# Weights rounded on ScalarE and their rest taken on VectorE, with a list scheduler that treats the path of VectorE and GpSimd as exclusive

## The chip, the cores and the metric

One NeuronCore of a Trainium2 chip runs the whole program in one launch. The metric is the device time in microseconds of that core, the median of several executions. TensorE is PE in the profile, VectorE DVE, ScalarE ACT, GpSimd POOL, and SyncE, which issues the DMAs, SP.

## What is computed

Two blocks of two layers each work on 512 tokens of 1024 features; the second has a context of 256 tokens beside them. In outline, from the reference:

```python
for l in range(2):                          # first block
    u = rms_norm(h, attn_norm[l])
    (dq, dk, dv, rq, rk, rv, rg, gq, gk, gv, gate_logits) = split(u @ w_in[l])
    a, r, c = differential_attention, bidirectional_retention, grouped_query_attention
    h = h + sum(sigmoid(gates) * projected(a, r, c)) @ w_out[l]
    h = h + square(relu(rms_norm(h, mlp_norm[l]) @ w_mlp_in[l])) @ w_mlp_out[l]
for l in range(2):                          # second block
    mx = split(silu(c) @ w_mod[l] + b_mod[l])          # the modulation, also for the context
    z = modulate(rms_norm(x, norm1_g[l]), mx[0], mx[1]) @ w_in_2[l]
    y = concat(fourier_mix, latent_attention, conformer_conv)   # of parts of z; 31 taps in the convolution
    x = x + mx[2] * (y @ w_o[l])
    x = x + mx[5] * mlp(modulate(rms_norm(x, norm2_g[l]), mx[3], mx[4]))
return rms_norm(x, final_norm_g)
```

## The kernel before

Features lie on the partitions and tokens in the columns. Every product is made of fp32r parts: an operand is split into a rounded part (hi) and the rest (lo), and three matmuls, hi by hi, hi by lo and lo by hi, are summed in PSUM. A weight comes as a chunk of 128 x 1024 fp32 (512 KB) into one of three `raw` tiles, is rounded into one `w` tile, and its rest goes into another (six `w` tiles, so three weights at a time). `wload` (L589) does that. For each weight in turn it takes the next letter of HI and of LO (L57, L58): by these, every second weight is rounded on ScalarE with its rest taken on VectorE, and the others are rounded and reduced on GpSimd:

```python
if HI[turn[0] % len(HI)] == "P":
    G.tensor_scalar(out=wh, in0=raw, scalar1=1.0, scalar2=0.0, op0=ALU.mult, op1=ALU.add)
else:
    S.activation(wh, raw, AF.Copy)
lo(wl, raw, wh, G if LO[turn[0] % len(LO)] == "P" else V)
```

A full weight serves 24 matmuls of 512 columns for the 512 tokens.

The program has eight phases (`phase`, L1670): for each layer of the first block a mixer (three kinds of attention, `mixer1`) and an output projection with the MLP (`mlp`, L808), then the same for the second block (`mixer2`). Beside the MLPs of the first block, VectorE makes the modulation of the second (`modulation`, L1224): for 48 chunks of the modulation's weights, one product with a row sum for each of one or two vectors (tiles `mraw` and `junk`). In the second block's mixers VectorE makes the convolution's taps (`taps`, L1299; tiles `cu` to `h`): 25 of the 31 for each of two feature blocks, the others being shared by ScalarE and GpSimd. In the attention (`attend`, L1455) VectorE takes the score's minimum (`s<-sc`) and the rests of the split weights (`r<-mm,r`), ScalarE the exponential and GpSimd the division. The rests of squares for the norms (`squares`, L651; tile `x`) lie mostly on GpSimd, and so do the squares of the MLP's hidden layer.

Nobody writes the order down by hand. The code records its steps, and at the end of a phase `Sched.run` (L270) orders them by a list scheduler: it simulates the five engines with a duration for each step (`_cost`, L484), gives each free engine its ready step of the lowest priority number, the number following the recorded order, and lets `hold` (L360) keep an engine free for a more urgent step that is about to come. Each engine's steps go on its queue in that order, and each waits for its inputs in the queue. In the model of before, VectorE and GpSimd do not hinder each other.

Of the kernel before, what the change touches and what calls it, by code (L numbers as in the profile page):

```python
# [56 lines left out]
HI = "AP"  # L57
LO = "VP"  # L58
# [26 lines left out]
class Buf:  # L85
    """A tile to be placed in one of its tag's slots."""
# [8 lines left out]
class View:  # L95
    """An access pattern on a Buf: the steps from the slot's tile, and what they give on the first slot."""
# [22 lines left out]
    def region(self):  # L119
        """bounds of the partitions and columns"""  # L120
        (pitch, n), *free = self.proto.ap
        p, c = divmod(self.proto.offset, pitch)
        return p, p + n, c, c + 1 + sum(abs(s) * (k - 1) for s, k in free)
# [8 lines left out]
class Op:  # L132
    __slots__ = ("eng", "calls", "cost", "prio", "idx", "bufs", "deps", "nexts", "ready", "unstarted", "soon", "allocs", "frees", "done", "line", "t0", "tr", "why", "rel", "slots", "outs")


class Tag:
# [4 lines left out]
    def take(self, pinned):  # L141
        """a free slot; what is kept beyond the phase goes into none of the phase's own"""
        for s in self.free:
            if (s in self.extra) != pinned:
                self.free.remove(s)
                return s
        return None if pinned else self.free.pop(0)


class Sched:  # L150
    """Records instructions on the engines, orders them by a model of the engines' time, issues them in that order."""

    def __init__(self, tc):
        self.tc, self.nc = tc, tc.nc
        self.tags, self.ops, self.bufs, self.bias, self.macro = {}, [], [], 0.0, None
        self.behind, self.dma = {}, 0.0
# [50 lines left out]
    def group(self):  # L207
        """the calls inside are one step of one engine"""
# [10 lines left out]
    def ahead(self, n):  # L219
        """the steps inside come before those recorded up to n steps earlier"""  # L220
# [11 lines left out]
    def _add(self, calls):  # L232
        op = Op()
        op.eng, op.calls, op.cost, op.idx = calls[0][0], calls, 0.0, len(self.ops)
        writes, reads, deps = [], [], {}
        for eng, name, a, k in calls:
# [7 lines left out]
            op.cost += _cost(eng, name, out, ins, k)  # L244
        for b, r in reads:
            deps.update((o.idx, o) for o, q in b.written if _meet(q, r))
        starts = any(k.get("start") for _, _, _, k in calls)
        for b, r in writes:
            # sums in one bank of PSUM come one after the other
# [20 lines left out]
    def run(self):  # L270
        """order and issue what has been recorded"""
        ops = self.ops
        total = len(ops)
        # how many slots of a tag are taken at each step of the recorded order
# [12 lines left out]
        if LS:  # L287
            # the latest start at which the tensor engine would not wait, were it to go in the recorded order
# [25 lines left out]
        ready = {e: [] for e in self.engines}  # L314
        events, order, now, dma = [(t, 0, 0) for t in sorted({0.0, *free_at.values()})], [], 0.0, self.dma
# [7 lines left out]
        def fits(b):  # L323
            """a slot is free, and taking it leaves enough for the steps before"""
# [35 lines left out]
        def hold(op):  # L360
            """when to look again, if a step that matters more comes before this one would be through"""
# [10 lines left out]
        while left:  # L372
            for e in self.engines:
                if free_at[e] > now:
                    continue
                while ready[e]:
# [6 lines left out]
                    if place(op):  # L383
# [4 lines left out]
                        else:  # L388
                            end = free_at[e] = now + op.cost
# [54 lines left out]
        # what is still under way when the tensor engine is through  # L444
        base = free_at["PE"]
        self.behind, self.dma = {e: max(0.0, t - base) for e, t in free_at.items()}, max(0.0, dma - base)
        for b in {id(b): b for b in self.bufs}.values():
            b.at = max(0.0, b.at - base)
# [34 lines left out]

def _cost(eng, name, out, ins, k):  # L484
    """an instruction's time in us, about"""
    n = max([_free_size(out)] + [_free_size(x) for x in ins if name in ("reduce_max", "tensor_reduce")])
    ps = any(_in_psum(x) for x in ins)
    if eng == "PE":
        if name == "transpose":
            return 0.115  # L490
        return n / 2400 + 0.0025 if n >= 256 else 0.22
# [16 lines left out]
def kernel(  # L508
# [80 lines left out]
    def wload(src, n=1024):  # L589
        """hi and lo of weights"""  # L590
# [17 lines left out]
    def prefetch(srcs):  # L608
        """weights for the next phase"""
# [6 lines left out]
    def gemm(w, off, nk, streams):  # L616
        """streams: (psum, hi blocks, lo blocks); w: hi and lo with block k at column off + k * 128."""
# [10 lines left out]
    def rstd(ms, eps, n=T):  # L628
        """-16/3 / sqrt(ms + eps) for rows that are alike: a guess from the bits, a step of third and one of second order on one copy"""
# [16 lines left out]
    def colsum(ps, m, x, start=True, stop=True):  # L646
        """the product of the symmetric constant m with x, given as its parts"""
# [39 lines left out]
    def qcol(p, name, n, scale):  # L687
        """gains of queries whose products are the negated scores"""
# [4 lines left out]
    def softmax(ps, e):  # L693
        """of the negated scores; less than normalized by the returned factor"""
# [10 lines left out]
    def sumsq(src, n):  # L705
        """the squares of all blocks but the last, summed"""
# [8 lines left out]
    def factor(most, last, n):  # L715
        """of the norm, from the squares' sum and the last block"""
# [5 lines left out]
    def operand(n):  # L722
        """hi and lo tiles of a block, kept until they are unpinned"""
# [5 lines left out]
    def cut(n):  # L729
        """the columns in halves, as far as they are more than 256"""  # L730
        return [slice(c, c + TC) for c in range(0, n, TC)]

    def scaled(y, x, gain, R, b):
        """x times its norm's factor; some of the blocks on another engine"""
# [7 lines left out]
    def norm_split(src, gains, n, shifts=None, over=False, later=None):  # L742
        """over: src is not needed any more; later: what is left to do for the last columns is put here"""
# [36 lines left out]
    def sweep(ws, streams, done, first=0, last=0):  # L780
        """products of each of the weights with the streams (hi blocks, lo blocks, n); done(unit, stream, columns, psum).
        The first units take the columns in halves as they come; the last ones finish one half before the other."""
# [953 lines left out]
    src = xT  # L1736
# [214 lines left out]
```

## Time and profile before

| | |
|---|---|
| runs shown | 3695.89, 3703.10, 3703.23 us; median 3703.1 |
| span of the profiled execution | 3698.5 us, 46918 instructions; the profile gives no other time of its own for it, and the three runs lie on both sides |
| mean granted clock of TensorE | 0.965 |
| PE | 3398.3 us busy (92%) |
| DVE | 2291.2 us (62%) |
| ACT | 1205.4 us (33%) |
| POOL | 1883.2 us (51%) |
| DMA | 324.48 MB, mean 88 GB/s |

Busy times are sums over the whole span, and the stages differ: an engine with a mean of 62% can be full in one of them. The first block's mixers run to about 620 and 1655 us, their MLPs to about 1060 and 2090; the second block's mixers, the third and the fourth, run to about 2400 and 3270, their MLPs to about 3030 and the end. All work is issued from one helper, so every row carries line L443; the rows are told apart by their tiles, with buffer numbers left out.

### The profile page before, as it was taken

The page shows a single profiled execution, that of the slowest core. Times are in us where ns is not written, and L with a number is a line of the kernel's source. Part 1 is how long each engine was busy: PE and PEld are TensorE (multiplying, and loading weights), DVE is VectorE, ACT ScalarE, POOL GpSimd, SP SyncE. Part 2 cuts the span into 40 slices and gives each one's busy share as a digit, 9 for nine tenths or more (in the row PEclk, how much of TensorE's full clock was granted, in tenths as well). Part 3 has the DMA queues.
Part 4 walks back from the last instruction along what each step waited for, and adds up shares of the span by engine and source line. Part 5 has one row for each costly group of instructions (what it writes and reads, how often), then busy time and mean ns, then how long its engine had stood idle before and what let it go on. Part 6 is the DMA issues. An engine that isn't in the chain of part 4 may idle for free. (4 is left out here: it accounts for less than half of the span.)

```text
span 3698.5 us, 46918 instructions
## 1 busy us (share of the span) xinstructions
PE 3398.3 (92%) x17724; PEld 2852.2 (77%) x17724; DVE 2291.2 (62%) x3816; ACT 1205.4 (33%) x2467; POOL 1883.2 (51%) x1350
## 2 busy tenths in 40 slices
PE   6999899899989998998999978899999987889998
PEld 5777677777877776777778867788888886878887
DVE  7777774998267778748842599852222259953223
ACT  3444332211234443333112326832111222742122
POOL 5544556554454445556544566643333346754445
PEclk9999999999989999999999989999999998999999
DMA  3221124454331211234743201121121221022332
GB/s 108 69 65 53 57 69 143 152 193 161 103 107 58 67 57 58 69 106 146 247 140 102 99 30 36 45 64 63 59 68 58 68 71 61 24 69 91 97 97 80
DMA packets 100308, 324.48 MB, mean 88 GB/s; under 512 B 11120, under 2 KB 18288, under 8 KB 100080
## 3 DMA queue, kind: packets, MB, share of 16 engines
q1 hardware_dynamic: 100080, 321.48, 26.2%
q8 instruction: 139, 2.28, 0.3%
q14 instruction: 89, 0.73, 0.1%
HBM read 312.00 MB, written 9.44 MB: 87 GB/s over the span
## 5 line engine op out<-in xcount | busy, mean ns | idle before, releaser
L443 PE MATMUL mm<-r,w 128*128 128x512 f32 (+2 forms) x12095 | 2604.5, 366 | 115.3 <-DVE r L443 50.2
L443 PEld LDWEIGHTS mm<-r,w 128*128 128x128 f32 (+1 forms) x12095 | 2060.2, 193 | 473.2 <-DVE r L443 60.3
L443 POOL TENSOR_TENSOR w<-raw,w 128x1024 fp32r<-128x1024 f32 (+1 forms) x232 | 676.4, 2915 | 725.7 <-PE mm L443 720.4
L443 DVE TENSOR_TENSOR w<-raw,w 128x1024 fp32r<-128x1024 f32 (+1 forms) x234 | 362.8, 1551 | 456.7 <-PE mm L443 406.1
L443 POOL TENSOR_SCALAR w<-raw 128x1024 fp32r<-128x1024 f32 (+1 forms) x232 | 268.0, 1155 | 534.0 <-PE mm L443 492.3
L443 ACT ACTIVATE w<-raw 128x1024 fp32r<-128x1024 f32 (+1 forms) x234 | 244.7, 1046 | 903.3 <-PE mm L443 662.8
L443 POOL TENSOR_SCALAR e<-e,s 128x512 f32<-128x512 f32 (+1 forms) x176 | 155.0, 885 | 176.6 <-DVE s L443 166.4
L443 ACT ACTIVATE e<-sc,s 128x512 f32<-128x512 f32 (+2 forms) x208 | 153.8, 741 | 144.2 <-DVE s L443 142.9
L443 DVE TENSOR_REDUCE s<-sc 128x1 f32<-128x512 f32 (+2 forms) x208 | 152.9, 741 | 36.8 <-PE sc L443 35.4
L443 PE MATMUL mm<-rc,w 128*128 128x256 f32 x768 | 166.1, 280 | 0.0
L443 PEld LDWEIGHTS mm<-rc,w 128*128 128x128 f32 x768 | 139.7, 188 | 20.5 <-POOL w L443 0.2
L443 DVE SCALAR_TENSOR_TENSOR mraw<-mraw,mrow 128x1024 f32<-128x1024 f32 x96 | 146.8, 1538 | 11.1 <-DMA mraw<-in_wmod_dram 7.8
L443 DVE SCALAR_TENSOR_TENSOR h<-cu,half,h 128x512 f32<-128x512 f32 (+1 forms) x144 | 151.7, 1083 | 1.5
L443 ACT ACTIVATE r<-t 128x512 fp32r<-128x512 f32 (+2 forms) x143 | 83.9, 592 | 141.5 <-DVE t L443 124.9
L443 PE MATMUL mm<-r,r 128*128 128x256 f32 (+1 forms) x592 | 115.5, 327 | 11.2 <-DVE r L443 8.1
L443 POOL TENSOR_TENSOR t<-t,t 128x512 f32<-128x512 f32 (+2 forms) x70 | 90.5, 1297 | 68.3 <-DVE t L443 44.7
L443 PE MATMUL mm<-x,sums 128*128 128x512 f32 (+1 forms) x152 | 62.9, 434 | 65.6 <-DVE sums L443 16.8
L443 ACT ACTIVATE r<-mm 128x256 fp32r<-128x256 f32 (+1 forms) x276 | 94.4, 404 | 72.9 <-PE mm L443 67.2
L443 PE MATMUL mm<-w,r 128*128 128x256 f32 x720 | 110.1, 298 | 8.2 <-DVE r L443 4.9
L443 ACT ACTIVATE t<-mm 128x512 f32<-128x512 f32 (+4 forms) x126 | 67.6, 538 | 150.3 <-PE mm L443 138.1
L443 DVE SCALAR_TENSOR_TENSOR junk<-mraw,mrow 128x1024 f32<-128x1024 f32 x64 | 116.1, 1815 | 0.6 <-DMA mraw<-in_wmod_dram 0.6
L443 DVE TENSOR_TENSOR r<-mm,r 128x256 fp32r<-128x256 f32 (+1 forms) x270 | 105.6, 432 | 10.9 <-ACT r L443 10.0
(586 smaller groups left out, 4511.7 us busy)
## 6 DMA issues: line engine op xcount, KB each, us to landing
raw<-in_wm_dram SPq DMA_DIRECT2D x256, 512.0 KB, 3.6
raw<-in_win_dram SPq DMA_DIRECT2D x134, 512.0 KB, 3.6
mraw<-in_wmod_dram SPq DMA_DIRECT2D x96, 512.0 KB, 4.1
raw<-in_wbr_dram SPq DMA_DIRECT2D x24, 512.0 KB, 3.5
raw<-in_wout_dram SPq DMA_DIRECT2D x16, 512.0 KB, 3.7
raw<-in_wo_dram SPq DMA_DIRECT2D x16, 512.0 KB, 3.4
kept<-h SPq DMA_DIRECT2D x24, 256.0 KB, 2.1
h<-kept SPq DMA_DIRECT2D x24, 256.0 KB, 4.6
```

The source lines that it names most:

```text
L443: getattr(self.engines[eng], name)(*[_real(x) for x in a], **{n: _real(x) for n, x in k.items()})
```

## The change

It has two parts. HI and LO lose their letter P: no weight is rounded or reduced on GpSimd any more; all are rounded on ScalarE, and all rests are taken on VectorE. And the scheduler keeps a time at which the common path of VectorE and GpSimd is free: a step that uses it starts in the model no earlier than that, and holds it to its end. By the new `_port`, every GpSimd step but a memset uses it, and on VectorE a step with two wide inputs in SBUF, or one of a few kinds with all inputs and the output in SBUF. TensorE's durations in the model change slightly too. The rest of the diff takes out comments and unused slots.

```diff
-HI = "AP"
-LO = "VP"
+HI = "A"
+LO = "V"
...
-        self.behind, self.dma = {}, 0.0
+        self.behind, self.dma, self.port = {}, 0.0, 0.0
...
+            op.port = op.port or _port(eng, name, out, ins)
...
+        port = self.port
...
-                            end = free_at[e] = now + op.cost
+                            end = free_at[e] = (max(now, port) if op.port else now) + op.cost
+                            if op.port:
+                                port = end
...
+        self.port = max(0.0, port - base)
...
+def _port(eng, name, out, ins):
+    if eng == "POOL":
+        return name != "memset"
+    if eng != "DVE" or name in ("memset", "reciprocal", "transpose", "stream_shuffle", "tensor_reduce", "reduce_max"):
+        return False
+    wide = [x for x in ins if not _in_psum(x) and _free_size(x) > 1]
+    return len(wide) > 1 or (len(wide) == len(ins) and not _in_psum(out) and name in ("tensor_scalar", "tensor_copy", "scalar_tensor_tensor"))
...
         if name == "transpose":
-            return 0.115
-        return n / 2400 + 0.0025 if n >= 256 else 0.22
+            return 0.11
+        return 0.009 + n * 0.000426 if n >= 256 else 0.22
```

The order on the engines, counted over the whole program: steps that write a weight's tile go from 234 to 466 on ScalarE, from 234 to 466 on VectorE and from 464 to none on GpSimd. No other kind of step is added or taken away on any engine; the matmuls are the same 17726 rows.

**VectorE beside the first MLP's second half of units** (`w<-raw,w` is a weight's rest, `mraw` and `junk` the modulation's products, `h<-h,mm` the residual's sum). Before:

```order
L443 TENSOR_TENSOR w_102<-raw_108,w_103 128x1024
L443 SCALAR_TENSOR_TENSOR mraw_4419,mod0c<-mraw_4419,mrow_4423 128x1024
L443 SCALAR_TENSOR_TENSOR junk_4424,mod0x<-mraw_4420,mrow_4422 128x1024
L443 TENSOR_TENSOR r_70<-t2x,r_71 128x512
L443 SCALAR_TENSOR_TENSOR mraw_4420,mod0c<-mraw_4420,mrow_4423 128x1024
L443 TENSOR_TENSOR h_139<-h_139,mm_4415 128x512
L443 SCALAR_TENSOR_TENSOR junk_4424,mod0x<-mraw_4421,mrow_4422 128x1024
L443 SCALAR_TENSOR_TENSOR mraw_4421,mod0c<-mraw_4421,mrow_4423 128x1024
L443 TENSOR_TENSOR w_106<-raw_108,w_107 128x1024
```

With the change:

```order
L447 TENSOR_TENSOR w_107<-raw_109,w_102 128x1024
L447 TENSOR_TENSOR h_142<-h_142,mm_4416 128x512
L447 SCALAR_TENSOR_TENSOR mraw_4420,mod0c<-mraw_4420,mrow_4423 128x1024
L447 SCALAR_TENSOR_TENSOR junk_4424,mod0x<-mraw_4421,mrow_4422 128x1024
L447 SCALAR_TENSOR_TENSOR mraw_4421,mod0c<-mraw_4421,mrow_4423 128x1024
L447 TENSOR_TENSOR w_103<-raw_110,w_106 128x1024
L447 TENSOR_TENSOR h_140<-h_140,mm_4417 128x512
L447 SCALAR_TENSOR_TENSOR junk_4424,mod0x<-mraw_4419,mrow_4422 128x1024
L447 SCALAR_TENSOR_TENSOR mraw_4419,mod0c<-mraw_4419,mrow_4423 128x1024
L447 SCALAR_TENSOR_TENSOR junk_4424,mod0x<-mraw_4420,mrow_4422 128x1024
L447 TENSOR_TENSOR w_107<-raw_108,w_105 128x1024
```

Before, a rest stood after every five products or so; now one stands after every two or three, and each residual's sum has one beside it. From the first product of this phase to its last stood 19 rests before and 46 now, so the 96 products are spread over more weights. In the second such phase (64 products) it is 15 and 33.

On GpSimd, where a rounding and a rest of a weight stood between the squares of the hidden layer, only the squares are left.

**VectorE in the third mixer, where the first score comes** (`h<-cu,half,h` a tap, `s<-sc` a score's reduction, `s<-s` a reciprocal, `q0l`, `q1l` and `r<-mm,r` parts of queries and of transposed scores). Before:

```order
L443 SCALAR_TENSOR_TENSOR h_145<-cu_14085,half,h_145 128x256
L443 SCALAR_TENSOR_TENSOR h_142<-cu_14084,half,h_142 128x256
L443 TENSOR_TENSOR r_100<-mm_14074,r_100 128x256
L443 SCALAR_TENSOR_TENSOR h_145<-cu_14085,half,h_145 128x256
L443 SCALAR_TENSOR_TENSOR h_142<-cu_14084,half,h_142 128x256
L443 SCALAR_TENSOR_TENSOR h_145<-cu_14085,half,h_145 128x256
L443 TENSOR_REDUCE s_133<-sc_14072 128x1
L443 TENSOR_REDUCE s_131<-sc_14073 128x1
L443 RECIPROCAL s_127<-s_134 128x1
```

With the change:

```order
L447 TENSOR_REDUCE s_127<-sc_14072 128x1
L447 TENSOR_TENSOR w_102<-raw_109,w_107 128x1024
L447 RECIPROCAL s_131<-s_129 128x1
L447 TENSOR_REDUCE s_123<-sc_14073 128x1
L447 TENSOR_REDUCE s_136<-sc_14072 128x1
L447 SCALAR_TENSOR_TENSOR h_140<-cu_14082,half,h_140 128x512
L447 RECIPROCAL s_135<-s_133 128x1
L447 SCALAR_TENSOR_TENSOR h_141<-cu_14083,half,h_141 128x512
L447 RECIPROCAL s_137<-s_125 128x1
L447 TENSOR_REDUCE s_128<-sc_14073 128x1
L447 TENSOR_TENSOR r_83<-mm_14077,r_72 128x2x128
```

Before, 80 of this mixer's 96 two-input taps stood ahead of the first score's reduction; now it is 37, and the other 59 stand among the 48 reductions, the last of them behind 38. In the fourth mixer, with 48 taps and 32 reductions, 41 stood ahead, and now 32 do.

## Rows read from the trace of the kernel before

**Rows 1.** The page, busy time by engine: us, share of the span, instructions.
```profile
PE 3398.3 (92%) x17724; PEld 2852.2 (77%) x17724; DVE 2291.2 (62%) x3816; ACT 1205.4 (33%) x2467; POOL 1883.2 (51%) x1350
```

**Rows 2.** Busy time by stretch: stretch and its us, engines, clock, DMA share, GB/s.
```profile
92.00:555.00 463.00, 435.35 (x2057) 339.39 (x2056) 350.41 (x653) 185.45 (x387) 233.04 (x159) 0.98 0.19 63
692.00:842.00 150.00, 132.51 (x569) 107.88 (x569) 147.64 (x166) 28.63 (x40) 73.95 (x38) 0.95 0.58 199
1760.00:1900.00 140.00, 122.88 (x506) 98.29 (x506) 109.71 (x132) 22.39 (x30) 65.70 (x32) 0.93 0.66 225
2117.00:2400.00 283.00, 229.74 (x1475) 200.84 (x1474) 266.02 (x508) 158.49 (x392) 187.68 (x176) 0.93 0.12 37
3055.00:3268.00 213.00, 176.72 (x1095) 155.16 (x1093) 196.50 (x338) 116.55 (x274) 147.86 (x120) 0.91 0.14 45
3346.00:3677.00 331.00, 331.00 (x1522) 276.72 (x1523) 83.66 (x95) 74.80 (x111) 169.91 (x103) 1.00 0.30 94
```

**Rows 3.** Weights: groups by shape (all), then durations in ns, 3345 to 3676.
```profile
L443 DVE TENSOR_TENSOR w<-raw,w 128x1024 fp32r<-128x1024 f32 x228 | 357.8, 1570 | 456.7 <-PE mm L443 406.1 <-issue 40.3 <-ACT w L443 10.1
L443 ACT ACTIVATE w<-raw 128x1024 fp32r<-128x1024 f32 x228 | 241.7, 1060 | 903.3 <-PE mm L443 662.8 <-DMA raw<-in_wm_dram 192.8 <-DMA raw<-in_win_dram 12.7
...
L443 DVE TENSOR_TENSOR w<-raw,w x31: 1224/1226/2811, 3344.6 to 3661.7; 128x1024 fp32r<-128x1024 f32 x31
...
L443 POOL TENSOR_TENSOR w<-raw,w x31: 2412/3146/3317, 3344.8 to 3668.2; 128x1024 fp32r<-128x1024 f32 x31
L443 POOL TENSOR_SCALAR w<-raw x30: 1055/1057/1378, 3351.7 to 3667.0; 128x1024 fp32r<-128x1024 f32 x30
```

**Rows 4.** Timeline: one collision of VectorE and GpSimd (start us, us, engine).
```profile
807.34 2.05 DVE L443 TENSOR_TENSOR w<-raw,w 128x1024 fp32r<-128x1024 f32 x1
808.28 3.37 POOL L443 TENSOR_TENSOR w<-raw,w 128x1024 fp32r<-128x1024 f32 x1
809.32 3.40 DVE L443 SCALAR_TENSOR_TENSOR mraw<-mraw,mrow 128x1024 f32<-128x1024 f32 x1
...
812.65 1.21 DVE L443 SCALAR_TENSOR_TENSOR junk<-mraw,mrow 128x1024 f32<-128x1024 f32 x1
...
813.80 0.68 DVE L443 TENSOR_TENSOR r<-t2x,r 128x512 fp32r<-128x512 f32 x1
```

**Rows 5.** Groups by shape, 690 to 850: VectorE, then GpSimd.
```profile
L443 DVE SCALAR_TENSOR_TENSOR junk<-mraw,mrow 128x1024 f32<-128x1024 f32 x34 | 61.8, 1817 | 0.0
L443 DVE SCALAR_TENSOR_TENSOR mraw<-mraw,mrow 128x1024 f32<-128x1024 f32 x34 | 50.7, 1491 | 0.5
L443 DVE TENSOR_TENSOR w<-raw,w 128x1024 fp32r<-128x1024 f32 x13 | 24.3, 1872 | 3.9 <-issue 3.9
...
L443 POOL TENSOR_TENSOR w<-raw,w 128x1024 fp32r<-128x1024 f32 x12 | 35.8, 2985 | 31.6 <-PE mm L443 31.6
```

**Rows 6.** TensorE's waits: 692 to 842; 1760 to 1900; 1665 to 1760; all.
```profile
PE mm L443 <- DVE r L443: 11.0, 3, 4.7
PE mm L443 <- DVE w L443: 6.5, 2, 4.9
...
PE mm L443 <- DVE r L443: 14.8, 6, 5.1
...
PE mm L443 <- POOL w L443: 5.6, 2, 2.8
...
PE mm L443 <- POOL x L443: 14.8, 15, 3.0
```

**Rows 7.** Taps: 2117 to 2400, 3055 to 3268; then score reductions, 2200 to 2420.
```profile
L443 DVE SCALAR_TENSOR_TENSOR h<-cu,half,h 128x512 f32<-128x512 f32 x48 | 51.6, 1100 | 0.8
L443 DVE SCALAR_TENSOR_TENSOR h<-cu,half,h 128x256 f32<-128x256 f32 x48 | 38.0, 823 | 0.4
...
L443 DVE SCALAR_TENSOR_TENSOR h<-cu,half,h 128x512 f32<-128x512 f32 x48 | 62.2, 1325 | 0.3
...
L443 DVE TENSOR_REDUCE s<-sc x48: 385/939/958, 2257.8 to 2391.8; 128x1 f32<-128x768 f32 x32, 128x1 f32<-128x256 f32 x16
```

More of the change, by code (lines that the diff above doesn't have):

```diff
@@ L132 @@
 class Op:
-    __slots__ = ("eng", "calls", "cost", "prio", "idx", "bufs", "deps", "nexts", "ready", "unstarted", "soon", "allocs", "frees", "done", "line", "t0", "tr", "why", "rel", "slots", "outs")
+    __slots__ = ("eng", "calls", "cost", "prio", "idx", "bufs", "deps", "nexts", "ready", "unstarted", "soon", "allocs", "frees", "done", "rel", "outs", "port")
 class Tag:
@@ L233, in _add @@
         op = Op()
-        op.eng, op.calls, op.cost, op.idx = calls[0][0], calls, 0.0, len(self.ops)
+        op.eng, op.calls, op.cost, op.idx, op.port = calls[0][0], calls, 0.0, len(self.ops), False
         writes, reads, deps = [], [], {}
```

## The prediction

> **What bounds the kernel now.** I began with busy time by engine: TensorE is busy 3398.3 of 3698.5 us, 92% [rows 1]. So nothing outside TensorE can give back more than the 300 us in which it stands, and the question is where these lie and who owes them. The next view was busy time by stretch. In the last MLP, 3346 to 3677, TensorE is busy all 331 us at a granted clock of 1.00, and VectorE 83.66 [rows 2]: half of its weights go through GpSimd there, and none is late. Nothing done to the weights can help such a stretch. In the first attention stage, 92 to 555, TensorE is busy 435.35 of 463 us. The idle time is thick in four other stretches of the same group: 692 to 842 and 1760 to 1900, the MLPs of the first block beside which VectorE computes the modulation, and 2117 to 2400 and 3055 to 3268, the second block's attention with the convolution's taps on VectorE. There VectorE is busy 147.64 of 150, 109.71 of 140, 266.02 of 283 and 196.50 of 213 us. In all four it is the engine to watch, and each names a wait on it below.
>
> **Why VectorE is so full there.** The same instruction has two very different times. The rest of a 1024-column weight on VectorE takes 1570 ns in the mean of 228, while in the last MLP its median is 1226 and its longest 2811; GpSimd's version of it runs from 2412 to 3317 there [rows 3]. The timeline of one collision shows why [rows 4]. VectorE's rest, noted at 807.34, ends at 809.39 although it needs 1.23; GpSimd's rest, noted at 808.28, ends at 811.65, which is some 2.3 after VectorE's end; VectorE's product noted at 809.32 takes 3.40 and ends at 812.72, one 1.2 after GpSimd's end; the next one, with nobody against it, takes 1.21. The two take turns, whole instruction by whole instruction. So in these stretches the thing that fills is their common path, and VectorE's busy time holds its waiting.
>
> **Part 1: 232 weights leave GpSimd.** Each took there a rounding of 1.06 us and a rest of 2.41 at best [rows 3], both through the common path: 3.47 us. Now it takes a rounding of 1.06 on ScalarE, which is busy 28.63 of 150 us in the fullest MLP stretch [rows 2], and a rest of 1.23 on VectorE. ScalarE's share I cost at nothing: its cover is the idle time of an engine that has over 110 us of 150 free, and in the attention of 2117 to 2400, where it is busy 158.49 of 283, nine more roundings are under 10 us. On VectorE the sum is 232 x 1.23 = 285 us of new work, against 3.47 - 1.23 = 2.2 us less on the common path for each weight.
>
> *The two modulation stretches.* From 690 to 850 VectorE's rows are 34 products of 1817 ns, 34 of 1491 and 13 rests of 1872, together 136.8 us, and GpSimd makes 12 rests in 35.8 [rows 5]. Without collisions the 68 products are 68 x 1.21 = 82.3 and the 13 rests 16.0 [rows 4, 3]; with GpSimd's 12 weights at 3.47, 41.6, the common path carries 140 of 160 us before any of the hidden layer's squares and rests. After the change it carries 82.3 + 25 x 1.23 = 113. VectorE itself goes from 136.8 to 113 in these rows though it does 12 rests more, because the long GpSimd instructions that it waited out are gone. The order shows moreover fewer products to a weight. TensorE waits 11.0 + 6.5 us for VectorE in the first of the stretches and 14.8 in the second [rows 6], 32.3 in all. I take three quarters, **-24 us**; the bounds are 0 (products ahead of a rest still hold it up) and -32. Along with it goes a slower clock: the granted clock is 0.95 and 0.93 of full in the two stretches, against 1.00 in the last MLP, where TensorE does not stop [rows 2]. That is at most 0.05 x 150 + 0.07 x 140 = 17 us, much of it in idle time; **-6**, bounds 0 and -17.
>
> *The start of the second such phase.* TensorE waits 5.6 us for two weights that GpSimd makes [rows 6]. Rounded and reduced in 1.06 + 1.23 rather than 1.06 + 2.41, they come earlier; late next are the residual's norm and VectorE's rests. **-4**, bounds 0 and -5.6.
>
> *GpSimd's other work.* In the attention stages it makes the rests of squares, and a weight's 3.47 us stands ahead of them in its queue. TensorE waits 14.8 us for these, 15 times [rows 6]. **-6**, bounds +10 (the 1.23 us rests now stand ahead of VectorE's score work instead) and -14.8.
>
> *The two convolution stretches.* Nine weights leave GpSimd between 2117 and 2400 and eight between 3055 and 3268, by a count of its rests there, three and two of them short: some 9 us of rests more on VectorE in each. The long taps take 1100 and 1325 ns in the mean [rows 7], where a 512-column step with nobody against it takes 0.68 [rows 4]: collisions cost them 48 x 0.42 = 20 us and 48 x 0.65 = 31. GpSimd's weights are about 30 of its 187.68 and 147.86 us [rows 2], a sixth to a fifth, so they caused some 4 and 6 us of that, and about 3 of the short taps'. Part 1 alone costs VectorE about +3 us in each stretch.
>
> **Part 2: the scheduler's model.** With the common path exclusive in its model, the order changes most at the taps. Before, 80 of the 96 taps of the third attention stand on VectorE ahead of its first score reduction, and the clock agrees: the reductions run from 2257.8 to 2391.8 [rows 7], 140 us after the stretch began. Now 37 do, and the other 59 lie between the steps of the attention. 43 taps at about 0.96 us, the mean of 1100 and 823, are 41 us of VectorE that come later. That is no gain by itself, since VectorE bounds both halves; what it can win is VectorE's idle time, 283 - 266.02 = 17 us, and 213 - 196.50 = 16.5 in the fourth attention, where the taps ahead of the first score go from 41 to 32 of 48. I take half, 17, less the 6 of part 1: **-11 us**. Bounds: +26 (the taps hold the scores up) and -40 (half of all the taps' collision time goes too, because the order sends the two engines apart). The longer TensorE step in the model, 0.227 for 0.216 us, moves fill work a little and has no row; nothing, inside these bounds.
>
> **Sum.** -24 - 6 - 4 - 6 - 11 = -51 us on the profiled span of 3698.5: 3647.5. The median of the runs shown, 3703.1, lies 4.6 above that span; the forecast for a median is 3652.
>
> A rule of the Trainium skill speaks against the change. Perfetto Trace Analysis, Optimizing Scalar/DVE Operations, advises, where VectorE is saturated, to take work away to ScalarE or even GpSimd, though it adds that the two share a port so that moving between them might not help. By its first half, bringing rests to a VectorE that is busy nine tenths would cost their whole time, which is the rival S below, +44 us where the sum says -51. The collision of rows 4 speaks for its second half, and I go by the sum.
>
> **The rivals.**
> S, slower: VectorE becomes the bound. It decides if a weight's share of VectorE in the modulation stretches exceeds the 5.3 us in which TensorE uses up a weight (331 us for the 62 whose rests start in the last MLP [rows 2, 3]). With three products, a rest and a 0.68 step it is 3 x 1.21 + 1.23 + 0.68 = 5.5, with two 4.3. The order holds both; over eight weights there are 20 products, 4.9 on average, so the margin is thin, and collisions with GpSimd's remaining squares could eat it. Then the new rests of the two stretches, 12 as GpSimd makes them in the first [rows 5] and as many assumed in the second, cost 1.23 each, 30 us, those of the convolution 18, and only the -4 is kept: +44, **3747**. Against it: the common path gets 27 us of 160 free. 10%.
> N, no change: the waits come from the products' places ahead in VectorE's queue, whoever shares its path. Then the products still hold up rests, the waits of 32.3 us stay, and so does the clock. -4 and -6 are left, and the taps win nothing: **3693**, or 3699 with part 1's 3 us in each of their stretches. For it: VectorE idles under 3 of 150 us. 12%.
> B, a larger gain: the model's order keeps the engines apart everywhere. -32 - 14 - 5.6 - 14.8 - 40 = -106: **3597**. For it: collisions touch nearly every two-input row of VectorE. Against: the order is set from modelled times, and the chip's drift from them. 18%.
>
> **How the numbers follow.** The forecast has 60%. Its bounds do not all fall together; -90 to -10 holds most of it. The range 3600 to 3697 leaves out S and about half of B's cases and a little of N. A measurement of this kernel can tell about 0.2%, 7.4 us, from no change. Faster by more: the forecast, B and nearly half of N, 0.83. Within: half of N and the edge of S, 0.07. Slower: 0.10, from S.
>
> **What would show it.** Right: rests on VectorE near 1.25 us in the mean of 466 and none of a weight on GpSimd; modulation products near 1.25 instead of 1.5 to 1.8; TensorE's waits for VectorE in the first modulation stretch down from 17.5 to under 6, and its clock there near 1; the first score reduction of the third attention some 30 us sooner after the first tap, the last one at most 10 sooner. Wrong: products that stay above 1.5 us, a TensorE that waits for a rest more often than now, or an attention that grows by as much as the taps ahead of it shrink.

## The result, and the profile after

The changed kernel takes 3542.7 us in the median (3539.3 to 3545.9) against 3699.5 (3694.3 to 3703.2) for the kernel before beside it: a ratio of 0.9579, 95% interval [0.9565, 0.9592]. That is 157 us less. The forecast was 51, and the time lies 57 us below the range's lower end.

The page of the changed kernel, busy time by engine (us, share of the span, instructions), beside [rows 1]:

```profile
PE 3348.9 (95%) x17724; PEld 2823.5 (80%) x17724; DVE 2285.2 (65%) x4048; ACT 1437.3 (41%) x2699; POOL 948.2 (27%) x886
```

The profiled span went from 3698.5 to 3537.5, by 161. TensorE's idle time went from 300.2 to 188.6 us, by 111.6, and its busy time, for the same matmuls, by 49.4. The second number is nearly all clock: its mean over the span rose from 0.965 to 0.977, and busy time times clock is 3279 before and 3272 after. VectorE took on 232 more instructions and is busy 6 us less.

Groups by shape of the kernel before, whole span (count, then busy us and mean ns), beside [rows 3] for the weights:

```profile
L443 DVE SCALAR_TENSOR_TENSOR mraw<-mraw,mrow 128x1024 f32<-128x1024 f32 x96 | 146.8, 1538 | 11.1 <-DMA mraw<-in_wmod_dram 7.8 <-POOL mrow L443 2.4
...
L443 DVE SCALAR_TENSOR_TENSOR junk<-mraw,mrow 128x1024 f32<-128x1024 f32 x64 | 116.1, 1815 | 0.6 <-DMA mraw<-in_wmod_dram 0.6
```

and of the changed kernel:

```profile
L447 DVE TENSOR_TENSOR w<-raw,w 128x1024 fp32r<-128x1024 f32 x455 | 577.9, 1276 | 736.4 <-issue 358.1 <-PE mm L447 263.8 <-ACT w L447 113.1
...
L447 DVE SCALAR_TENSOR_TENSOR mraw<-mraw,mrow 128x1024 f32<-128x1024 f32 x96 | 129.8, 1362 | 4.4 <-DMA mraw<-in_wmod_dram 3.1
...
L447 DVE SCALAR_TENSOR_TENSOR junk<-mraw,mrow 128x1024 f32<-128x1024 f32 x64 | 82.1, 1283 | 0.0
```

A rest fell from 1570 to 1276 ns, near the 1226 that it takes undisturbed, and the products from 1538 and 1815 ns to 1362 and 1283. ScalarE took all roundings at the old price, 1058 ns.

To see where the time went I cut both spans at the residual's first and last sums, which bound each MLP. Busy time by stretch of the kernel before (stretch and its us; TensorE, its weight loads, VectorE, ScalarE, GpSimd; granted clock; DMA share; GB/s): first mixer, first MLP, second mixer, second MLP, third and fourth mixer.

```profile
0.00:623.20 623.20, 558.89 (x2674) 441.81 (x2675) 450.05 (x822) 240.92 (x500) 317.73 (x226) 0.98 0.22 73
623.20:1058.40 435.20, 404.77 (x1930) 340.46 (x1928) 307.20 (x380) 98.06 (x162) 236.70 (x140) 0.97 0.45 153
1058.40:1658.80 600.40, 554.74 (x2670) 440.11 (x2671) 443.92 (x805) 231.08 (x478) 300.42 (x207) 0.97 0.21 70
1658.80:2097.00 438.20, 406.60 (x1933) 340.65 (x1931) 250.45 (x340) 104.66 (x180) 233.72 (x145) 0.96 0.45 152
2097.00:2414.10 317.10, 262.39 (x1686) 231.72 (x1687) 285.07 (x565) 170.47 (x419) 199.56 (x189) 0.92 0.15 47
3029.00:3284.20 255.20, 208.56 (x1257) 183.06 (x1258) 225.68 (x406) 131.83 (x306) 160.82 (x135) 0.89 0.16 51
```

The same six stretches of the changed kernel:

```profile
0.00:582.90 582.90, 547.11 (x2672) 435.13 (x2673) 437.58 (x859) 275.85 (x537) 173.95 (x153) 0.99 0.23 79
582.90:984.10 401.20, 392.87 (x1932) 333.86 (x1930) 286.05 (x414) 132.21 (x197) 76.78 (x67) 0.99 0.50 165
984.10:1545.70 561.60, 541.63 (x2667) 434.69 (x2668) 427.64 (x841) 265.00 (x514) 163.79 (x136) 0.98 0.22 76
1545.70:1948.60 402.90, 395.44 (x1936) 335.86 (x1934) 247.83 (x373) 140.21 (x215) 74.02 (x72) 0.99 0.48 165
1948.60:2265.90 317.30, 264.65 (x1686) 230.62 (x1687) 275.53 (x577) 182.87 (x430) 168.54 (x170) 0.95 0.14 48
2878.50:3125.90 247.40, 207.36 (x1258) 179.98 (x1259) 216.28 (x422) 143.38 (x317) 129.20 (x117) 0.91 0.16 54
```

Length less TensorE's busy time is its idle time. The two MLPs with the modulation gave 34 and 35 us (idle 30 to 8 and 32 to 7, the rest clock). The first block's mixers gave 40 and 39, which the forecast had hardly counted: idle time 64 to 36 and 46 to 20. The mixers with the convolution gave nothing and 8, the last two MLPs 2 and 3.

TensorE's waits in the first MLP (us in total, times, longest), before:

```profile
PE mm L443 <- DVE r L443: 14.8, 5, 4.7
PE mm L443 <- DVE w L443: 8.1, 4, 4.9
PE mm L443 <- POOL w L443: 2.3, 1, 2.3
...
```

and after:

```profile
PE mm L447 <- DVE w L447: 3.7, 1, 3.7
PE ms L447 <- DVE x L447: 3.2, 2, 1.6
...
```

The wait for the hidden layer's parts on VectorE [rows 6] is gone.

### The profile page after: what moved, and what is told of

Same layout as the page of the kernel before. It is cut to its first block, busy times and chain, and to the rows that moved or that the text cites. A ratio compares the mean times of both kernels' runs of the same rounds, so it can differ in the third digit from the quotient of the medians.

```text
span 3537.5 us, 46905 instructions
## 1 busy us (share of the span) xinstructions
PE 3348.9 (95%) x17724; PEld 2823.5 (80%) x17724; DVE 2285.2 (65%) x4048; ACT 1437.3 (41%) x2699; POOL 948.2 (27%) x886
## 4 chain that ended last, share of the span: by engine, by line
PE 85%; DVE 9%; ACT 3%; issue 2%; POOL 1%; DMA 0%; SPq 0%; DVEq 0%; ACTq 0%; POOLq 0%
PE mm L447 79%; PE sc L447 5%; DVE r L447 2%; DVE h L447 2%; PE acc L447 2%; DVE w L447 1%; DVE s L447 1%; DVE t L447 1%; ACT r L447 1%; ACT e L447 1%; DMA raw<-in_win_dram 0%; ACT t L447 0%; ACT w L447 0%; POOL t L447 0%; POOL h L447 0%
## 5 line engine op out<-in xcount | busy, mean ns | idle before, releaser
L447 PE MATMUL mm<-r,w 128*128 128x512 f32 (+1 forms) x12134 | 2570.7, 363 | 55.1 <-DVE w L447 23.0
L447 PEld LDWEIGHTS mm<-r,w 128*128 128x128 f32 x12134 | 2041.9, 191 | 399.7 <-DVE w L447 26.2
L447 DVE TENSOR_TENSOR w<-raw,w 128x1024 fp32r<-128x1024 f32 (+1 forms) x466 | 588.0, 1268 | 736.4 <-issue 358.1
L447 ACT ACTIVATE w<-raw 128x1024 fp32r<-128x1024 f32 (+1 forms) x466 | 483.7, 1046 | 1042.1 <-PE mm L447 900.8
L447 DVE SCALAR_TENSOR_TENSOR mraw<-mraw,mrow 128x1024 f32<-128x1024 f32 x96 | 129.8, 1362 | 4.4 <-DMA mraw<-in_wmod_dram 3.1
L447 POOL TENSOR_TENSOR x<-t,x 128x512 fp32r<-128x512 f32 (+1 forms) x58 | 82.5, 1425 | 175.1 <-ACT x L447 175.1
L447 DVE SCALAR_TENSOR_TENSOR h<-cu,half,h 128x512 f32<-128x512 f32 (+1 forms) x144 | 122.6, 865 | 0.8
L447 ACT ACTIVATE r<-t 128x512 fp32r<-128x512 f32 (+3 forms) x141 | 84.2, 601 | 87.9 <-DVE t L447 66.0
L447 PEld LDWEIGHTS mm<-r,r 128*128 128x128 f32 x595 | 96.9, 202 | 25.8 <-ACT r L447 6.7
L447 PEld LDWEIGHTS mm<-w,r 128*128 128x128 f32 x736 | 98.3, 195 | 11.6 <-DVE w L447 5.3
L447 DVE TENSOR_TENSOR r<-t,r 128x512 fp32r<-128x512 f32 (+2 forms) x117 | 91.8, 791 | 13.1 <-ACT r L447 10.4
```

What stands on the lines that cost most here:

```text
L447: getattr(self.engines[eng], name)(*[_real(x) for x in a], **{n: _real(x) for n, x in k.items()})
```

## The experiments

My theory C: what the weights on GpSimd cost was the common path, on which VectorE's two-input instructions stood behind GpSimd's. Its rivals: Q, the cost was GpSimd's own queue, in which other work stood behind a weight; and O, the gain is the new model's order and not the move. In the expectations M stands for the move, against O. Lengths of the phases, in us by the cuts above (of one profiled execution each), with the median time and its ratio to the kernel before:

| kernel | median | ratio | mixer 1 | MLP 1 | mixer 2 | MLP 2 | mixer 3 | MLP 3 | mixer 4 | MLP 4 |
|---|---|---|---|---|---|---|---|---|---|---|
| before | 3699.5 | 1 | 623 | 435 | 600 | 438 | 317 | 615 | 255 | 402 |
| changed | 3542.7 | 0.958 | 583 | 401 | 562 | 403 | 317 | 613 | 247 | 399 |
| move alone | 3535.0 | 0.956 | 591 | 400 | 574 | 402 | 304 | 608 | 242 | 399 |
| model alone | 3587.9 | 0.970 | 595 | 401 | 573 | 406 | 333 | 609 | 259 | 399 |
| before's order, weights moved | 3602.5 | 0.974 | 608 | 409 | 584 | 421 | 312 | 611 | 242 | 400 |
| changed order, weights back | 3653.6 | 0.988 | 599 | 425 | 584 | 424 | 327 | 615 | 256 | 402 |
| changed + extra reads | 3656.1 | 0.988 | 606 | 427 | 584 | 422 | 331 | 614 | 259 | 401 |
| changed + extra fills | 3561.6 | 0.963 | 588 | 401 | 573 | 403 | 323 | 608 | 249 | 400 |
| roundings alone moved | 3685.2 | 0.996 | 623 | 426 | 601 | 430 | 330 | 612 | 248 | 401 |
| model in mixers 1, 2 only | 3524.8 | 0.952 | 587 | 400 | 568 | 402 | 306 | 608 | 241 | 398 |

**The two parts apart.** The move alone is the kernel before with two letters taken out:

```diff
-HI = "AP"
-LO = "VP"
+HI = "A"
+LO = "V"
```

> The kernel before with HI and LO alone changed: the scheduler of before plans with all weights on ScalarE and VectorE, and knows nothing of a common path. Theory M (the gain comes from the weights' leaving GpSimd): 3545 to 3590 us, at least 70% of the gain of 157. Theory O (the gain comes from the order that the new model makes): 3640 to 3680. If each half is needed: 3590 to 3640.

Measured: 3535.0, ratio 0.9559 [0.9545, 0.9573]. The model alone is the changed kernel with the letters put back:

```diff
-HI = "A"
-LO = "V"
+HI = "AP"
+LO = "VP"
```

> The changed kernel with HI and LO as before: every second weight is made on GpSimd, and the scheduler plans with the exclusive path and the new TensorE durations. Theory M: 3670 to 3705 us. Theory O: 3560 to 3620, with the modulation stretches as tight as in the changed kernel.

Measured: 3587.9, 0.9703 [0.9688, 0.9717]. The move alone gives 163 us, all of the gain and a little over. The model alone gives 110, but on top of the move it costs 8, at the edge of what the intervals tell apart. O falls as the explanation of the whole. But the model alone came in O's range and far below M's, so the order is a second way to much of the gain, and not by sparing VectorE collisions. In the first MLP, the rests of the kernel before, then those of the model alone and its busy time (columns as above):

```profile
L443 DVE TENSOR_TENSOR w<-raw,w 128x1024 fp32r<-128x1024 f32 x35 | 66.5, 1900 | 44.1 <-PE mm L443 40.2 <-issue 3.9
```

```profile
L447 DVE TENSOR_TENSOR w<-raw,w 128x1024 fp32r<-128x1024 f32 x36 | 93.4, 2593 | 36.8 <-issue 19.6 <-PE mm L447 16.9 <-ACT w L447 0.3
```

```profile
594.80:995.80 401.00, 394.27 (x1922) 333.83 (x1920) 334.01 (x376) 96.75 (x159) 227.94 (x136) 0.99 0.48 165
```

A rest takes longer than before and VectorE is fuller (334 us for 307), yet TensorE stands only 7 us, for 30: its wait for the hidden layer's parts on VectorE fell from 14.8 us to 1.3. So there it is the order of VectorE's work, and not fewer collisions, that frees TensorE.

**The model's two numbers apart.** With the letters as before, the model was given only TensorE's new times, or only the path:

```diff
-            op.port = op.port or _port(eng, name, out, ins)
+            op.port = False
```

> The kernel before with TensorE's durations in the model alone changed (0.227 us for a 512-column matmul in place of 0.216). The two models together, without the move, gave 3588 us. Theory D (the durations do it: the model had TensorE too fast, so that it hurried fill work and put the rest late): 3585 to 3620. Theory E (the exclusive path does it): 3680 to 3710.

Measured: 3753.3, 1.0148 [1.0128, 1.0168]: a little slower than before.

```diff
-            return 0.11
-        return 0.009 + n * 0.000426 if n >= 256 else 0.22
+            return 0.115
+        return n / 2400 + 0.0025 if n >= 256 else 0.22
```

> The kernel before with the exclusive path alone in the model. Theory D: 3670 to 3710 us. Theory E: 3580 to 3620.

Measured: 3640.4, 0.9839 [0.9824, 0.9855]. Then the same two edits to the changed kernel as it is, with the weights moved. Only TensorE's times:

> The changed kernel without the exclusive path in the model: weights moved, new TensorE durations. The move alone gave 3535 us and the whole change 3543. If the path is what costs the third mixer 13 us over the move alone: 3515 to 3535, that mixer again about 304 us. If the durations cost it: 3540 to 3550, that mixer about 317.

Measured: 3585.6, 0.9693 [0.9678, 0.9708]. Only the path:

> The changed kernel with TensorE's old durations in the model: weights moved, exclusive path. If the path costs the third mixer its 13 us: 3540 to 3560 us, that mixer about 317. If the durations do: 3525 to 3540, that mixer about 304.

Measured: 3565.5, 0.9642 [0.9626, 0.9658]. Against the kernel before (ratios times 3699.5), with its weights: TensorE's times +55, the path -60, both -110. With the weights moved: neither -163, times -114, path -132, both -156. These don't add up, no single number is the model's worth, and none of the four lies in a range that I expected. The third mixer, of which two of them asked, took with the weights moved 304 us with neither, 314 with the times, 334 with the path and 317 with both. Why TensorE's times alone make a worse order than the old ones stays open.

**The order held fixed.** Before's order to the last instruction, but what is planned for GpSimd is issued on ScalarE and VectorE:

```diff
+                out = k.get("out")
+                if eng == "POOL" and isinstance(out, View) and out.buf.tag == "w":
+                    if name == "tensor_scalar":
+                        self.engines["ACT"].activation(_real(out), _real(k["in0"]), AF.Copy)
+                        continue
+                    eng = "DVE"
```

> The kernel before, planned exactly as before with every second weight on GpSimd, but at the issue such a weight's rounding goes to ScalarE and its rest to VectorE, at the same place in the list. Theory M: 3550 to 3600 us, since the collisions and GpSimd's queue are relieved whatever the order. Theory O: 3660 to 3720, VectorE taking 285 us of rests in an order that did not expect them.

Measured: 3602.5, 0.9742 [0.9727, 0.9756]. The converse: planned as the changed kernel, but every second weight's instructions issued on GpSimd (`back` holds the tiles of every second weight).

```diff
+                out = a[0] if a else k.get("out")
+                if isinstance(out, View) and id(out.buf) in self.back:
+                    if eng == "ACT":
+                        self.engines["POOL"].tensor_scalar(out=_real(out), in0=_real(a[1]), scalar1=1.0, scalar2=0.0, op0=ALU.mult, op1=ALU.add)
+                        continue
+                    if eng == "DVE":
+                        eng = "POOL"
...
```

> The changed kernel, planned as changed, but at the issue every second weight goes back to GpSimd, at the same place in the list. Theory M: 3660 to 3720 us, the first-block mixers again about 600 us each. Theory O: 3570 to 3620.

Measured: 3653.6, 0.9882 [0.9866, 0.9899]. So the engines alone, in the same order, give 95 us one way and cost 111 the other; letting the old planner know of the move gives 67 more. Both times lie just outside M's ranges, on M's side.

Not all of the 95 us go through VectorE. From the kernel before to its order with the weights moved, TensorE's waits over the whole span fell from 288 to 216 us: those for VectorE from 194 to 145, those for GpSimd from 33 to 10. In the converse TensorE waits for GpSimd's own weights, which are late in an order that expects them sooner. TensorE's waits for these over the whole span, before and in the changed order with the weights back:

```profile
PE mm L443 <- POOL w L443: 9.5, 5, 2.8
```

```profile
PE mm L454 <- POOL w L454: 40.4, 25, 5.1
```

So a weight's own lateness on GpSimd is a cost beside C and Q, small in the kernel before and larger in the converse.

In the second mixer the shares of engines and order can be told apart. TensorE's waits there, before:

```profile
...
PE sc L443 <- DVE r5x L443: 7.7, 1, 7.7
PE mm L443 <- POOL x L443: 4.5, 5, 1.9
PE mm L443 <- DVE s L443: 4.0, 1, 4.0
...
```

with before's order and the weights moved:

```profile
...
PE sc L449 <- DVE r5x L449: 5.9, 1, 5.9
...
```

and in the changed kernel:

```profile
PE mm L447 <- DVE w L447: 7.2, 2, 5.0
...
PE mm L447 <- POOL x L447: 0.8, 1, 0.8
...
```

The move takes away the waits for GpSimd's rests of squares and for one late step of a norm (`s`). The wait for a part on VectorE ahead of the scores (`r5x`) stays while the order stays; it is gone in the changed kernel, and still 4.1 us in the move alone.

**Path or queue.** To the changed kernel, whose order knows nothing of it, GpSimd work is added beside every second full weight's rest, which nothing waits for. Once it reads SBUF:

```diff
...
+                        for _ in range(4):
+                            self.engines["POOL"].tensor_tensor(out=self.scratch, in0=self.scratch, in1=self.scratch, op=ALU.add)
```

> The changed kernel; beside every second weight's rest GpSimd adds a 352-column scratch tile to itself four times, some 3.8 us, which nothing waits for. Theory C (what the weights on GpSimd cost was the common path: VectorE's instructions stood behind GpSimd's): modulation products rise again to about 1.5 to 1.8 us and the time to 3580 to 3650. Theory Q (the cost was GpSimd's own queue: its rests of squares and probabilities stood behind a weight): the same rise, but the kernel with fills of equal length rises as much.

Measured: 3656.1, 0.9878 [0.9863, 0.9893]. And once it only writes:

```diff
...
+                        for _ in range(10):
+                            self.engines["POOL"].memset(self.scratch, 0.0)
```

> As the one with extra reads, but GpSimd fills the scratch tile ten times instead, some 3.8 us without reading. Theory C: VectorE's instructions keep their times (modulation products about 1.36 us) and the time stays at 3535 to 3560. Theory Q: as slow as the one with extra reads, 3580 or more.

Measured: 3561.6, 0.9625 [0.961, 0.9639]. The groups of VectorE and GpSimd with extra reads:

```profile
L447 DVE TENSOR_TENSOR w<-raw,w 128x1024 fp32r<-128x1024 f32 x455 | 631.3, 1394 | 660.9 <-issue 338.9 <-PE mm L447 215.0 <-ACT w L447 102.1
L447 DVE SCALAR_TENSOR_TENSOR mraw<-mraw,mrow 128x1024 f32<-128x1024 f32 x96 | 144.2, 1511 | 5.8 <-DMA mraw<-in_wmod_dram 4.7
...
L447 DVE SCALAR_TENSOR_TENSOR junk<-mraw,mrow 128x1024 f32<-128x1024 f32 x64 | 100.6, 1572 | 0.0
...
L453 POOL TENSOR_TENSOR scratch<-scratch 128x352 f32<-128x352 f32 x912 | 984.0, 1079 | 58.5
```

with extra fills:

```profile
L447 DVE TENSOR_TENSOR w<-raw,w 128x1024 fp32r<-128x1024 f32 x455 | 577.5, 1275 | 731.3 <-issue 356.2 <-PE mm L447 267.2 <-ACT w L447 106.6
L447 DVE SCALAR_TENSOR_TENSOR mraw<-mraw,mrow 128x1024 f32<-128x1024 f32 x96 | 130.6, 1370 | 3.5 <-DMA mraw<-in_wmod_dram 2.2
...
L447 DVE SCALAR_TENSOR_TENSOR junk<-mraw,mrow 128x1024 f32<-128x1024 f32 x64 | 81.9, 1279 | 0.0
...
L453 POOL MEMSET scratch<- 128x352 f32 x2280 | 897.6, 394 | 121.4
```

GpSimd is loaded with 900 to 980 us either way. Reads cost 113 us, as much as the weights themselves when put back; fills cost 19 and leave these durations of VectorE's where they were, to 8 ns. Both times lie a few us above C's ranges. The timeline of the kernel with reads shows the mechanism on one stretch (start us, us, engine):

```profile
803.16 12.70 POOL L453 TENSOR_TENSOR scratch<-scratch 128x352 f32<-128x352 f32 x8
803.67 1.79 DVE L447 SCALAR_TENSOR_TENSOR junk<-mraw,mrow 128x1024 f32<-128x1024 f32 x1
...
805.39 1.78 DVE L447 TENSOR_TENSOR w<-raw,w 128x1024 fp32r<-128x1024 f32 x1
807.10 1.79 DVE L447 SCALAR_TENSOR_TENSOR mraw<-mraw,mrow 128x1024 f32<-128x1024 f32 x1
...
814.01 1.21 DVE L447 SCALAR_TENSOR_TENSOR mraw<-mraw,mrow 128x1024 f32<-128x1024 f32 x1
```

While GpSimd works off eight additions in a row, VectorE's first three two-input instructions of 1024 columns take 1.78 to 1.79 us instead of 1.21. Not each is held up: the one at 814.01 takes 1.21. So added GpSimd work costs its reading far more than its place in the queue, and C is a sufficient cause of a loss of this size. Of the 19 us only a part is traced to Q, in TensorE's waits for GpSimd's rests of squares over the whole span, with fills and then without:

```profile
PE mm L447 <- POOL x L447: 7.4, 9, 1.9
```

```profile
PE mm L447 <- POOL x L447: 2.7, 4, 0.8
```

The Trainium skill has this on its page SBUF — State Buffer, section Who interferes with whom: an instruction of VectorE with two inputs in SBUF contends with a GpSimd instruction that reads SBUF, and not with one that only writes it. The two runs agree, 1572 against 1279 ns for the `junk` products.

**Roundings alone moved.** Here only HI lost its P:

```diff
-HI = "AP"
+HI = "A"
```

> The kernel before with all roundings on ScalarE, every second rest still on GpSimd, the old model. Theory C: a weight's relief of the common path is 3.47 - 1.23 = 2.24 us with the whole move and 1.06 with the rounding alone, 47%, so of the 163 us that the move alone gives some 77 come: about 3621. Theory R (only the two-input rests collide, the rounding never held VectorE up): 3680 to 3700. Theory A (the rounding was what hurt, since it comes first in the chain and the rest waits for it): 3560 or less.

Measured: 3685.2, 0.9956 [0.9942, 0.997]. The miss is C's, as I had priced it by time on the path: the time fell by 0.44%, some 16 us, and not by 77. It lies in the range of R (only the rests collide). The groups show what stayed:

```profile
L443 DVE TENSOR_TENSOR w<-raw,w 128x1024 fp32r<-128x1024 f32 x228 | 331.1, 1455 | 513.7 <-PE mm L443 413.2 <-ACT w L443 63.8 <-issue 36.3
...
L443 DVE SCALAR_TENSOR_TENSOR mraw<-mraw,mrow 128x1024 f32<-128x1024 f32 x96 | 151.9, 1589 | 12.4 <-DMA mraw<-in_wmod_dram 11.1
...
L443 DVE SCALAR_TENSOR_TENSOR junk<-mraw,mrow 128x1024 f32<-128x1024 f32 x64 | 97.4, 1522 | 0.1
```

Of VectorE's rows the rests (1570 to 1455 ns) and the `junk` products (1815 to 1522) shortened part of the way, the `mraw` products (1538 to 1589) did not. VectorE is busy 54 us less over the span (2291.2 to 2237.5) and TensorE stands only 14 us less, so VectorE's relief doesn't become time one for one. R's ground isn't so: in the trace of the kernel before, VectorE's 388 rests and products of 1024 columns take 152 us beyond 1.21 us each. Of these, 105 us fall on instructions that overlap a rest on GpSimd, and 27 on those that overlap a rounding there and no rest; one that overlaps a rounding alone takes up to 2.06 us. By this count the long two-input rest weighs most; what the roundings are worth in the kernel's time isn't separated, as the order differs too in this run.

**A better mixture.** The phases of the table suggested the new model for the first block's mixers alone:

```diff
-            op.port = op.port or _port(eng, name, out, ins)
+            op.port = op.port or NEW[0] and _port(eng, name, out, ins)
...
+        NEW[0] = name.startswith("m1")
```

(and TensorE's times by the same flag).

> The changed kernel with the new model (common path and TensorE times) in the first block's mixers alone, the old model in all other phases. If the phases are independent, the time is put together from those already measured: first-block mixers of the changed kernel (582.9 + 561.6), all the rest from the kernel with the move alone (399.8 + 401.8, 304.1 + 608.4 + 242.1 + 398.7, 12 after them): 3511 us, faster than the changed kernel (3542.7) and than the move alone (3535.0). Rival: what a phase's order gains is handed over from the one before (weights loaded early, work left behind), so the mixture gives no more than the better of the two, 3530 to 3545.

Measured: 3524.8, 0.9523 [0.9509, 0.9538], the fastest here, and apart from the move alone (0.9545 to 0.9573). It lies between the sum of phases, 3511, and the rival's range. The first two mixers came at 587 and 568 instead of 583 and 562. For the first this is no handing over between phases, as none stands before it: with the same order on VectorE, ScalarE and GpSimd up to its end, TensorE was 2.4 us behind by then. Lengths of single phases are therefore good to a few us, and why the sum was missed stays open.

## Why the prediction was right and where it was wrong

**Right** were the direction and, in the modulation stretches, the mechanism: collisions on the common path lengthen VectorE's instructions there, and the move takes most of that away although VectorE does more. Of its checks, rests came at 1276 ns, `junk` products at 1283 and the clock of the modulation's MLPs at 0.99; the `mraw` products stayed at 1362. Wait terms came too: the start of the second MLP (-4 forecast; TensorE waits for no weight of GpSimd any more), and GpSimd's rests of squares (14.8 to 2.7 us over the whole span).

**The first failed step is "GpSimd's other work", -6.** I had costed the first block's mixers by TensorE's waits for GpSimd alone, with a bound of -14.8, and let VectorE's waits there stand. They gave 40 and 39 us; less the 6, that is two thirds of the 110 us that the sum was short on the span. The sign was in the trace. A weight's rest took 1873 ns on VectorE in the second mixer, as long as in the modulation stretch [rows 5], and 1310 after. Groups by shape of the kernel before, 1058 to 1658 us, and of the changed one, 984 to 1545:

```profile
L443 DVE TENSOR_TENSOR w<-raw,w 128x1024 fp32r<-128x1024 f32 x36 | 67.3, 1873 | 20.4 <-PE mm L443 20.0 <-ACT w L443 0.3
```

```profile
L447 DVE TENSOR_TENSOR w<-raw,w 128x1024 fp32r<-128x1024 f32 x71 | 92.5, 1310 | 29.5 <-PE mm L447 21.0 <-ACT w L447 4.2 <-issue 4.1
```

VectorE was busy 350 of 463 us in the first mixer's stretch [rows 2], and the collisions there got no term. With the order held, the move gave 15 and 17 us in the two mixers; planned anew by the old model it gave 32 and 26, and the new model without the move gave 28 and 27. So a part of the 79 is collisions and GpSimd's queue, and the larger part needs a new order; why that order gains so much there stays open. The length of a rest doesn't size it: in the second mixer it is 1332 ns with the order held and 1711 with the model alone, which is 11 us shorter. Of the first mixer's 28 us of idle time, 9 lie in the first 92 us (35.4 to 26.7), a stretch that the prediction left out.

**The modulation stretches were undersized.** -24, -6 and -4 make 34; the two MLPs gave 69. I had cut windows of 150 and 140 us out of phases of 435 and 438, and summed waits over these alone: 32.3 us for VectorE, while TensorE's idle time in the two whole phases is 62. It fell to 16.

**The clock, -6, was the third step that failed.** Over the span TensorE's busy time fell by 49 us, of which 23 in those two MLPs and 25 in the first two mixers. I had taken it as a small share of the granted clock's distance from full; it was 0.44 us for each us of idle time that went (49.4 / 111.6).

**The convolution, -11, came near (0 and -8) by two errors.** Part 1 was put at +6, and the move alone gave -13 in each of the two mixers (304 and 242 for 317 and 255; with the order held -5 and -13). Part 2, the model, was put at -17, and on top of the move it cost 13 and 5 (317 and 247 for 304 and 242). That the total came near is luck. The score reductions of the third mixer, changed kernel and then the move alone (ns min/median/max, first and last start):

```profile
L447 DVE TENSOR_REDUCE s<-sc x48: 386/940/959, 2076.2 to 2240.1; 128x1 f32<-128x768 f32 x32, 128x1 f32<-128x256 f32 x16
```

```profile
L443 DVE TENSOR_REDUCE s<-sc x48: 378/940/958, 2111.2 to 2246.7; 128x1 f32<-128x768 f32 x32, 128x1 f32<-128x256 f32 x16
```

and the two-input taps, of the kernel before and the changed one:

```profile
L443 DVE SCALAR_TENSOR_TENSOR h<-cu,half,h x96: 460/752/2775, 2117.6 to 2294.8; 128x256 f32<-128x256 f32 x48, 128x512 f32<-128x512 f32 x48
```

```profile
L447 DVE SCALAR_TENSOR_TENSOR h<-cu,half,h x96: 456/740/1840, 1968.3 to 2204.3; 128x256 f32<-128x256 f32 x48, 128x512 f32<-128x512 f32 x48
```

From the first tap, the first score is reduced after 108 us in the changed kernel, where it was 140 before; the last after 272, where it was 274 [rows 7]. The reductions now take 164 us instead of 134. So the first score came 32 us sooner, as the prediction said, and the attention grew by 30, nearly as much as the taps ahead of it shrank, which it had named as the sign of being wrong. With the move alone they take 136.

**The rivals.** S (VectorE becomes the bound) is refuted: with more instructions VectorE is busy less. N (the waits come from the products' places in VectorE's queue) is refuted in its number, and half right in its reason: the new order alone, with the weights left on GpSimd and VectorE fuller, brought the two modulation MLPs to 401 and 406 us. B was 54 us too few, because it too left the first mixers and the clock at the bounds of their windows. Its reason, that the model's order keeps the engines apart everywhere, isn't what happened: the move gave the gain without the model, and the model alone lengthened the rests (1782 ns in the mean of the span, for 1570). The rule of the Trainium skill (Perfetto Trace Analysis, Optimizing Scalar/DVE Operations) that the prediction weighed advises taking work off a saturated VectorE, and adds that moving it between VectorE and GpSimd might not help, as they share a port. The second half is what the runs bear out: here moving work to the fuller of the two gave 163 us.

## What to carry to other kernels

Where GpSimd works beside VectorE, price its instructions by what they hold up: a two-input instruction of VectorE that comes behind a long one of GpSimd's can wait it out (3.40 us for 1.21 [rows 4]), in phases too where VectorE's mean load leaves room. Then ask what waits for VectorE: the order alone took TensorE's waits away with the collisions still there. Size a gain over whole phases, not over the worst window, and add the clock's share of the idle time that goes. And judge a change of a planner's model per phase: the same model won in two mixers and lost in two others.

## What was not expected of the hardware

GpSimd's fills left VectorE's `junk` products at 1279 ns, where additions of a similar total length took them to 1572. And with 112 us of TensorE's idle time went 49 us of its busy time for the same matmuls, nearly all by the clock (3279 and 3272 us of busy time times clock), though the mean granted before was 0.965 already.
